# Hybrid decoder layer on one core: later conditioning loads moved and made larger, offsets on the recurrence's products in the planner

## The chip, the cores and the metric

The kernel runs on one core of a Trainium2 chip. The metric is device time in microseconds (us); the profile is one execution, taken by the hardware profiler. TensorE (PE) does the matrix products, VectorE (DVE), ScalarE (ACT) and GpSimd (POOL) the rest, and SyncE (SP) issues nearly all DMAs, one after the other from one queue.

## The reference, cut to what matters

One layer over T = 1024 prompt tokens and 8 sample tokens (1032 columns), D = 1024, float32:

```python
mod = silu(c) @ w_ada + b_ada              # shift1, scale1, gate1, shift2, scale2, gate2
h = rms_norm(x) * (1 + scale1) + shift1
u_glu, qkv_raw, z, b_raw, a_raw, gate_a, gate_b = split(h @ w_in)
# branch A: GLU -> causal depthwise conv (31) -> LayerNorm -> silu -> w_conf_out
# branch B: conv (4) + silu on q, k, v -> gated delta rule, 8 heads of 128 x 128
#           -> rms_norm * silu(z) -> w_gdn_out
merged = sigmoid(gate_a) * y_a + sigmoid(gate_b) * y_b
x = x + gate1 * (merged @ w_o)
h2 = rms_norm(x) * (1 + scale2) + shift2
x = x + gate2 * (relu(h2 @ w_ff1) ** 2 @ w_ff2)
```

The samples have states of their own (the last rows of both convolutions, and one delta matrix for each head), which are read and written back.

## The kernel before, in words

Every large product is done with operands split into a high and a low part (`hi`, `lo`): three products, hi*hi, hi*lo and lo*hi, stand for one. A weight tile comes as 256 KB pieces `raw` (two for an input projection tile); ACT casts each to `whi`, POOL subtracts to get `wlo`. A tile of 128 outputs by 1032 tokens is 72 matmuls of 344 columns (`mm`), in groups of three.

The order of the program is not written by hand. The code records operations (`Op`) with a priority (`plan.prio`, lower goes first), and `Plan.run` plays them through on estimated costs: an engine that is free takes the ready operation of the lowest priority whose tiles fit in their rings. What comes out is a fixed order for each engine, and the chip runs each in that order, with semaphores between engines. If an input is later on the chip than in the plan, the engine stands there, and everything behind it too. `ready` sets when an operation counts as ready (`op.avail`): the end of the latest predecessor and a gap by engine.

Tiles live in rings: `P4`, 34 slots of 4 KB a partition (large tiles), `P2`, 21 slots of 2 KB, and `PS`, the eight PSUM banks. `caps` says how many slots a class may take.

The work in the order of the span:

- Input norm, transposes, and the first part of the conditioning (`ada_first`, 32 loads `wk` of 256 KB), which gives shift1 and scale1. The shifted `h` (`Hh`, `Hl`) is complete at about 57 us.
- The input projection, 56 tiles: for each head k, q and v (`qkv_tile`), the conformer's two (`conformer`), and gates z, gb, ga. Between them the recurrence: 16 units (`unit`: 8 heads, two halves), each one long chain of small products and evictions: transposes (`tT`), `kq`, a triangular inverse in steps (`i16`, `i32`, `j32`, `j64`, `k64`, `k64b`, `k128`; the profile cuts the numbers off, so `i`, `j`, `k`), and four steps of `py`, `pd`, `pw` (each with `po`, the output) that carry the state. PE has dense matmuls of the projection in between, as the plan puts them.
- `ba`, `cum`, `cumT`: decay sums that each unit needs, through DRAM (`scrG`, `Gb`, `glb`).
- `ada_round(1)` and `(2)`: the rest of the conditioning, 64 loads `wk` of 256 KB in the small ring (class `raw`, nine slots, the same as for weights), priority 900. Its result `modT` is first used in the output projection.
- Convolution of 31 taps on DVE (`conf_conv`), the samples' delta step (`pks`, `s0`, `delta_sample`), LayerNorm sums (`pmean`, `pvar`).
- `w_gdn_out` products, `w_conf_out` products, the output projection `w_o` in token quarters (0, 2 and then 1, 3), with `norm2` behind it: `hr` (normed rows), and `parts` of sums and differences (`t1`, `t2`, `bp`) for the feed-forward, which is two products by a seven-product scheme (`ff`), from about 1260 us to the end.

All engine calls go through one line of `Plan.run`, so the profile shows every instruction at one line (469), and one goes by names: out<-in.

Of the kernel before, what the change touches and what calls it, by code (L numbers as in the profile page):

```python
# [10 lines left out]
ALU = mybir.AluOpType  # L11
AX = mybir.AxisListType
# [126 lines left out]


class Op:
    __slots__ = ("alts", "prio", "idx", "tiles", "preds", "succs", "npred", "avail", "start", "eng", "fin", "table", "done", "soft")


ENG = ("PE", "ACT", "DVE", "POOL", "SP")
HOP = 0.4
GAP = {"SP": 0.95, "DVE": 0.127, "POOL": 0.1, "ACT": 0.15}
TABLE = {AF.Exp: "exp", AF.Silu: "silu", AF.Tanh: "", AF.Sqrt: "sqrt"}

# [8 lines left out]
class Plan:  # L158
# [60 lines left out]
    def add(self, alts, reads, writes):  # L219

        op = Op()
        op.alts, op.prio, op.idx, op.done = alts, self.prio, self.n, False
        self.n += 1
        op.preds, op.succs, op.tiles, op.table = set(), [], [], None
        for calls, _ in alts.values():
            for m, a, k in calls:
                if m == "activation":
                    f = a[2] if len(a) > 2 else k.get("func")
                    op.table = TABLE.get(f) or None
        seen = set()  # L230
        for w, refs in ((False, reads), (True, writes)):
            for r in refs:
                for q, box, qw in r.t.acc:
                    if (w or qw) and q is not op and _overlap(box, r.box):
                        op.preds.add(q)
        for w, refs in ((False, reads), (True, writes)):
            for r in refs:
                if w:
                    r.t.acc = [x for x in r.t.acc if not all(c <= a and b <= d for (a, b), (c, d) in zip(x[1], r.box))]
                r.t.acc.append((op, r.box, w))  # L240
                if r.t not in seen:
                    seen.add(r.t)
                    op.tiles.append(r.t)
                    r.t.left += 1
        for t in self.touch:
            if t not in seen:
                seen.add(t)
                op.tiles.append(t)
                t.left += 1
        self.touch = ()  # L250
        op.soft = set(self.after) - op.preds
        op.preds.update(self.after)
        self.after = ()
        self.last = op
        op.preds = [q for q in op.preds]
        self.ops.append(op)
        return op
# [80 lines left out]
    def run(self, name=""):  # L338
# [12 lines left out]
        def ready(op):  # L351
            nonlocal seq
            op.avail = 0.0
            for q in op.preds:
                if q in op.soft:
                    op.avail = max(op.avail, q.start)
                    continue
                same = len(op.alts) == 1 and q.eng in op.alts and q.eng != "SP"
                op.avail = max(op.avail, q.fin + (0.0 if same and q.eng == "PE" else GAP.get(q.eng, HOP)))
            seq += 1  # L360
            heapq.heappush(events, (op.avail, seq, op))
            if len(op.alts) == 1:
                for e in op.alts:
                    soon[e].append(op)
# [11 lines left out]
        while todo:  # L376
# [8 lines left out]
            for e in ENG:  # L385
# [4 lines left out]
                for x in cand[e]:  # L390
# [3 lines left out]
                    k = x.prio  # L394
                    if e == "ACT" and x.table and self.tab and x.table != self.tab:
                        k += self.switch
                    k = (k, x.idx)
# [13 lines left out]
                op = best  # L411
# [46 lines left out]
        for op in sorted(order, key=lambda o: (o.start, o.idx)):  # L458
            for x in op.tiles:
                if x.ap is None:  # L460
                    ring, i = x.slot
# [5 lines left out]
            h = self.hw[op.eng]  # L467
# [13 lines left out]
def hybrid(tc, I, O):  # L481
    nc = tc.nc
    with ExitStack() as ctx:
        ctx.enter_context(tc.manual_schedule())

        def pool(name, space=None, st=ctx, **k):
# [11 lines left out]
            xin=("P4", 16), u=("P4", 8), wk=("P2", 15), h=("P4", 16), w=("P4", 4), wl=("P4", 8), sqa=("P2", 4), rawq=("P4", 2), qkv=("P4", 6),  # L498
            gt=("P4", 3), glu=("P4", 1), av=("P4", 1), avl=("P4", 4), s0=("P4", 3), a=("P4", 8), o=("P4", 16),
            g=("P4", 16), x1=("P4", 8), h2=("P4", 28), hr0=("P4", 6), hr1=("P4", 6), wc=("P4", 7), wd=("P4", 8), wo=("P4", 6), fb=("P4", 18), bp=("P2", 4),  # L500
            acc=("P4", 10), cs=("P4", 2), ff=("PS", 8),
            raw=("P2", 9), Gb=("P2", 2), ktok=("P2", 2), vtok=("P2", 1), att=("P2", 2), Dm=("P2", 1),
            Am=("P2", 1), kqs=("P2", 4), otok=("P2", 2), oT=("P2", 2), tmp=("P2", 12), one=("P2", 19), sq=("P2", 3), lsq=("P2", 4))
        for c, n in dict(jk=2, A32=1, Ad=1, Ao=2, Ac=1, Tc=1, Tb=2, T32=1, Tt=2, Pt=2, Ut=1, R=2, vn=2, Sn=3, st=2, s8=8,
# [123 lines left out]
        def ada_round(r):  # L628
            ps = bank("x", "ada")
            for c in range(4):  # L630
                cols = slice(c * 128, c * 128 + 128)
                for k in range(8):
                    wk = tl("raw", [128, 4, 128], "wk")
                    SP.dma_start(wk, I["w_ada"][4 * r + c, k].rearrange("p (j n) -> p j n", j=4))
                    if k == 0 and c == 0:
                        plan.touch = (ps,)
                    with plan.group("PE"):
                        for j in range(4):
                            TE.matmul(ps[32 * j:32 * j + 32, cols], lhsT=cT[:, k, :], rhs=wk[:, j], start=(k == 0), stop=(k == 7),
                                      tile_position=(0, 32 * j))  # L640
            mo = tl("one", [128, 512], "mo")
            copy(mo, ps)
            ps2 = bank("x", "adaT")
            for c in range(4):
                TE.transpose(ps2[:, c * 128:(c + 1) * 128], mo[:, c * 128:(c + 1) * 128], ident)
            V.tensor_tensor(
                modT[:, 16 * r - 16:16 * r, :].rearrange("p (j c) b -> p j c b", c=4),
                ps2.rearrange("p (c j b) -> p j c b", c=4, j=4)[:, :, :, 0:9],
                bada[:, 16 * r:16 * r + 16].rearrange("p (j c) -> p j c", c=4).unsqueeze(3).to_broadcast([128, 4, 4, 9]),
                ALU.add)  # L650
# [188 lines left out]
        for t in Ub:  # L839
            P.memset(t, 0.0)  # L840

        pk_last = [None]

        def qkv_tile(m, c, i):
            raw = tl("rawq", [128, SL], "rawq")
# [242 lines left out]
            (mm_k if (c, i) == ("ga", 7) else mm)(hi, lo, 8, hx, lambda ns, ps, n: A.activation(gt[:, ns], ps, func, scale=scl))  # L1088
            A.dma_start(spl[c][i], gt)

        plan.prio = 60
        cstT = tl("cs", [128, 4, 8, 30], "cstT")
        plan.after = (ada_op,)
        SP.dma_start(cstT, I["csT"])
        for i in range(4):
            V.tensor_tensor(cstT[:, i], cstT[:, i], cdw[:, 0:30, i].unsqueeze(1).to_broadcast([128, 8, 30]), ALU.mult)
        csS = const([128, 4, 8], "csS")
        V.tensor_reduce(csS, cstT, axis=AX.X, op=ALU.add)
        V.tensor_scalar(cdw, cdw, 0.5, None, op0=ALU.mult)

        av_op = [None]
        conv_after = ()
# [27 lines left out]
            SP.dma_start(aD[i], av)  # L1130
            av_op[0] = plan.last

        plan.prio = 3000
        plan.after = (ada_op,)
        SP.dma_start(O["conf_old"], I["state_conf_conv"][0, :, 1:30, :])
        plan.after = (ada_op,)
        SP.dma_start(O["qkv_old"], I["state_qkv_conv"][0, :, 1:3, :])
        for h in range(H):
            plan.prio = 100 * h + 25
            cur = [qkv_tile(b + h, c, h) for b, c in ((8, "k"), (0, "q"), (16, "v"))]  # L1140
            plan.prio = 100 * h + 20
            for hf in range(2):
                unit(h, hf, cur[1], cur[0], cur[2])
# [164 lines left out]
        plan.prio = 2500  # L1308
        w_g = I["w_gdn_out"]
        for m in range(8):  # L1310
            hi, lo = wload(w_g[m], 8, after=(chain[0],))

            def ev(ns, ps, n):
                sb = tl("tmp", [128, NG], "sb")
# [91 lines left out]
        def norm2(q):  # L1406
# [9 lines left out]
            for i in range(2):  # L1416
# [5 lines left out]
                if q == 3:  # L1422
                    us, ks = r[:, :, e:QW], slice(4 * i, 4 * i + 4)
                    V.tensor_tensor(us, us, s2[:, ks, 1:9], ALU.mult)
                    V.tensor_tensor(us, us, modT[:, 8 + 4 * i:12 + 4 * i, 1:9], ALU.add)
                SP.dma_start(x1D[q][i], x1[q][i])
            sh = [128, 4, QW]
            if q < 2:
                hB[c][1] = parts("h2", hr[0, 0], sh)
# [382 lines left out]
```

## Time and profile before

| | |
|---|---|
| median of 3 runs | 1948.68 us (1948.6 to 1950.59) |
| the profiled execution | 1951.48 us, span 1949.8 us |
| PE, DVE, ACT, POOL busy | 94%, 74%, 44%, 44% |
| DMA | 261.47 MB, mean 134 GB/s |
| granted PE clock, mean | 0.979 |

A wait is read like this: the profile counts an engine as idle before an instruction and names what released it ("2.07 <-DVE xa": idle for 2.07 us until DVE's `xa` was done). A matmul counts as busy longer than the time after which the next one can start, so short waits do not show.

### The profile page before, as it was taken

What the parts mean: (1) busy time and instruction counts of PE and PEld (TensorE: products, weight loads), DVE (VectorE), ACT (ScalarE), POOL (GpSimd) and SP (SyncE); (2) the same over time, 40 slices, a digit from 0 to 9 for tenths busy, and PEclk for the clock granted to TensorE, in tenths of its full rate; (3) what the DMA queues carried; (4) which work ended last, traced back from release to release, by engine and by line L of the source; (5) the groups of instructions that cost most, each with busy time, mean ns of one, the idle gap of its engine ahead of it and who ended that gap; (6) DMA issues with size and microseconds to landing.
All of it is one profiled execution on the core that took longest, in us unless ns stands there. A gap on an engine that the chain in (4) does not pass through costs nothing. (4 is left out here: it accounts for less than half of the span.)

```text
span 1949.8 us, 42076 instructions
## 1 busy us (share of the span) xinstructions
PE 1835.7 (94%) x16205; PEld 1752.1 (90%) x16205; DVE 1439.5 (74%) x3127; ACT 852.6 (44%) x2100; POOL 853.8 (44%) x735
## 2 busy tenths in 40 slices
PE   7899889998999899999999999899999999999995
PEld 4899778988888787999989999889999999999995
DVE  5414457777878998899964485985656677999997
ACT  5323334454545544621142125465555565343334
POOL 3313224354534644363323134422222238888874
PEclk9999899998999999999999999899999999999998
DMA  9441332011111103973254666234544574544432
GB/s 363 118 156 59 103 99 78 30 45 57 41 39 58 67 21 138 339 244 118 107 194 145 187 179 209 98 120 129 163 132 139 161 256 137 177 162 155 131 120 87
DMA packets 164700, 261.47 MB, mean 134 GB/s; under 512 B 27764, under 2 KB 91388, under 8 KB 164484
## 3 DMA queue, kind: packets, MB, share of 16 engines
q1 hardware_dynamic: 158740, 241.91, 38.7%
q10 hardware_dynamic: 5760, 16.88, 2.2%
q8 instruction: 127, 2.08, 0.4%
q14 instruction: 73, 0.60, 0.1%
HBM read 189.76 MB, written 69.64 MB: 133 GB/s over the span
## 5 line engine op out<-in xcount | busy, mean ns | idle before, releaser
L469 PE MATMUL mm<-h_hi,whi 128*128 128x344 f32 x1344 | 462.9, 344 | 4.5 <-ACT whi L469 4.5
L469 PE MATMUL mm<-h_hi,wlo 128*128 128x344 f32 x1344 | 434.7, 323 | 4.6 <-POOL wlo L469 4.4
L469 PE MATMUL mm<-h_lo,whi 128*128 128x344 f32 x1344 | 434.0, 323 | 0.3 <-DVE h_lo L469 0.3
L469 POOL TENSOR_TENSOR wlo<-raw,whi 128x512 fp32r<-128x512 f32 x168 | 248.7, 1495 | 334.7 <-ACT whi L469 242.8
L469 PE MATMUL ff<-fbh,wp 128*128 128x258 f32 x1808 | 331.0, 284 | 3.5 <-DVE accu L469 1.7
L469 PE MATMUL ff<-bp,wp 128*128 128x258 f32 x2688 | 326.7, 284 | 3.9 <-DVE bp L469 1.9
L469 PEld LDWEIGHTS ff<-bp,wp 128*128 128x128 f32 x2688 | 324.9, 190 | 5.4 <-DVE bp L469 2.1
L469 PEld LDWEIGHTS ff<-fbh,wp 128*128 128x128 f32 x1808 | 281.6, 190 | 7.0 <-DVE accu L469 2.8
L469 PEld LDWEIGHTS mm<-h_hi,whi 128*128 128x128 f32 x1344 | 256.5, 191 | 15.5 <-ACT whi L469 5.4
L469 PEld LDWEIGHTS mm<-h_hi,wlo 128*128 128x128 f32 x1344 | 255.9, 190 | 7.7 <-POOL wlo L469 7.6
L469 PE MATMUL ff<-fbl,wp 128*128 128x258 f32 x904 | 256.4, 284 | 2.4 <-DVE fbl L469 2.4
L469 PEld LDWEIGHTS mm<-h_lo,whi 128*128 128x128 f32 x1344 | 257.0, 191 | 0.5 <-DVE h_lo L469 0.5
L469 POOL TENSOR_TENSOR wp<-raw,wp 128x512 fp32r<-128x512 f32 x93 | 141.6, 1528 | 233.7 <-ACT wp L469 227.5
L469 DVE SCALAR_TENSOR_TENSOR av<-gl,vecs,av 128x1024 f32<-128x1024 f32 x120 | 183.4, 1528 | 2.3
L469 PEld LDWEIGHTS ff<-fbl,wp 128*128 128x128 f32 x904 | 171.5, 190 | 2.8 <-DVE fbl L469 2.8
L469 ACT CAST wp<-raw 128x512 fp32r<-128x512 f32 x159 | 95.6, 615 | 134.4 <-PE ff L469 55.2
L469 POOL TENSOR_TENSOR fbl<-fbl,fbh 128x516 fp32r<-128x516 f32 x100 | 149.4, 1528 | 9.8 <-issue 7.7
L469 ACT CAST whi<-raw 128x512 fp32r<-128x512 f32 x168 | 98.9, 619 | 115.0 <-DMA raw<-w_gdn_out 46.8
L469 DVE TENSOR_TENSOR ft<-ff,ft 128x258 f32<-128x258 f32 x160 | 67.4, 422 | 92.2 <-PE ff L469 91.2
L469 ACT ACTIVATE ft<-ft 128x258 f32<-128x258 f32 x224 | 93.4, 419 | 73.4 <-DVE ft L469 69.5
L469 PE MATMUL mm<-g_hi,whi 128*128 128x258 f32 x256 | 75.1, 293 | 6.8 <-ACT whi L469 5.4
L469 POOL TENSOR_TENSOR wp<-s,wp 128x512 fp32r<-128x512 f32 x31 | 51.1, 1650 | 68.1 <-ACT wp L469 68.1
(397 smaller groups left out, 3605.3 us busy)
## 6 DMA issues: line engine op xcount, KB each, us to landing
raw<-w_ff SPq DMA_DIRECT2D x128, 256.0 KB, 4.4
fD<-ft SPq DMA_DIRECT2D x228, 129.0 KB, 3.0
fbl<-fD SPq DMA_DIRECT2D x57, 516.0 KB, 3.6
raw<-w_in SPq DMA_DIRECT2D x112, 256.0 KB, 4.7
wk<-w_ada SPq DMA_DIRECT2D x96, 256.0 KB, 5.1
raw<-w_o SPq DMA_DIRECT2D x32, 256.0 KB, 3.9
sp_z<-gt ACTq DMA_DIRECT2D x8, 516.0 KB, 8.3
zt<-sp_z SPq DMA_DIRECT2D x24, 172.0 KB, 4.0
```

The lines of the kernel that those rows point to most:

```text
L469: getattr(h, m)(*[x.real() if isinstance(x, Ref) else x for x in a], **{q: x.real() if isinstance(x, Ref) else x for q, x in k.items()})
```

## The change

Five edits:

- The planner gives a product's non-PE inputs an offset (`MARGIN`, by the name of the tile written, 0.4 us for dense matmuls and the units' products, 1 to 5 us for others): such a product counts as ready that much later. It holds for PE operations of priority 10 to 2450 and for those of priority -2 and below. The plan puts other work in front; no wait is added on the chip.
- `ada_round` loads 32 pieces of 512 KB (two k blocks each) into two tiles of the large ring (class `ada`), held until the first head's v projection has been issued (`v_op`), with 16 products to a piece. The conformer state `csT` and the two state copies (`conf_old`, `qkv_old`) wait for the same.
- The first `w_gdn_out` tile is loaded at priority 2300 in place of 2500.
- The `parts` of `norm2(0)` and `norm2(2)` get priority 2701 in place of 2690, behind the output projection (2700); those of `norm2(1)` and `norm2(3)` stay at 2691.
- `op.margin` is one more field of `Op`.

```diff
+MARGIN = dict(cum=4.0, cumT=2.0, ada=5.0, adaT=2.0, sn=2.0, pdot=2.0, pks=3.0, pksT=1.0, son=2.0, vrT=2.0, pmean=4.0, pvar=4.0,
+              mm=0.4, **{n: 0.4 for n in ("tT", "kq", "i16", "i32", "j32", "j64", "k64", "k64b", "k128", "pw", "py", "pd", "po")})
...
+        late = "PE" in alts and not -2 < self.prio < 10 and self.prio < 2450
+        op.margin = max([MARGIN.get(r.t.name, 0.0) for r in writes], default=0.0) if late else 0.0
...
-                op.avail = max(op.avail, q.fin + (0.0 if same and q.eng == "PE" else GAP.get(q.eng, HOP)))
+                gap = 0.0 if same and q.eng == "PE" else GAP.get(q.eng, HOP)
+                op.avail = max(op.avail, q.fin + gap + (op.margin if q.eng != "PE" else 0.0))
...
-            acc=("P4", 10), cs=("P4", 2), ff=("PS", 8),
+            acc=("P4", 10), cs=("P4", 2), ff=("PS", 8), ada=("P4", 2),
...
-                for k in range(8):
-                    wk = tl("raw", [128, 4, 128], "wk")
-                    SP.dma_start(wk, I["w_ada"][4 * r + c, k].rearrange("p (j n) -> p j n", j=4))
+                for k2 in range(4):
+                    wk = tl("ada", [128, 2, 4, 128], "wk")
+                    plan.after = (v_op[0],)
+                    SP.dma_start(wk, I["w_ada"][4 * r + c, 2 * k2:2 * k2 + 2].rearrange("k p (j n) -> p k j n", j=4))
...
+        def conf_state():
+            cstT = tl("cs", [128, 4, 8, 30], "cstT")
+            plan.after = (v_op[0],)
+            SP.dma_start(cstT, I["csT"])
...
             cur = [qkv_tile(b + h, c, h) for b, c in ((8, "k"), (0, "q"), (16, "v"))]
+            if h == 0:
+                v_op[0] = pk_last[0]
+                plan.prio = 160
+                conf_state()
+                plan.prio = 3000
+                for o, i in (("conf_old", I["state_conf_conv"][0, :, 1:30, :]), ("qkv_old", I["state_qkv_conv"][0, :, 1:3, :])):
+                    plan.after = (v_op[0],)
+                    SP.dma_start(O[o], i)
...
         for m in range(8):
+            plan.prio = 2300 if m == 0 else 2500
             hi, lo = wload(w_g[m], 8, after=(chain[0],))
+            plan.prio = 2500
...
                 SP.dma_start(x1D[q][i], x1[q][i])
+            plan.prio = 2701 if c == 0 else 2691
             sh = [128, 4, QW]
```

What this does to the orders, at three places. First SP's queue in the opening, from the last loads of `ada_first` (`wk` ahead of and behind `alb`) to the decay sums' copies; `raw` is a piece of a projection weight. Before:

```order
L469 DMA alb<-ab 128x16
L469 DMA wk<-w_ada 128x512 x20
L469 DMA raw<-w_in 128x512 x2
L469 DMA cstT<-csT 128x960
L469 DMA conf_old<-state_conf_conv 8x14848
L469 DMA wk<-w_ada 128x512
L469 DMA qkv_old<-state_qkv_conv 8x6144
L469 DMA raw<-w_in 128x512 x4
L469 DMA wk<-w_ada 128x512 x6
L469 DMA scrS<-sab 8x16
```

Now, at the same place:

```order
L475 DMA alb<-ab 128x16
L475 DMA wk<-w_ada 128x512 x3
L475 DMA raw<-w_in 128x512 x2
L475 DMA wk<-w_ada 128x512 x6
L475 DMA raw<-w_in 128x512 x8
L475 DMA scrS<-sab 8x16
```

Nine of the `wk` belong to `ada_first` in both; the other eighteen, `csT` and both state copies have left this place, and four more weight pieces stand in it.

Second PE in a unit, the step from `py` to `pd` (DVE's `vn` lies between them) at the start of the fourth head's recurrence. Before:

```order
L469 MATMUL py<-vtok,U_78 128x128
L469 MATMUL mm<-h_hi_694,whi 128x344
L469 MATMUL mm<-h_lo_709,whi 128x344
L469 MATMUL mm<-h_hi_694,wlo 128x344
L469 MATMUL mm<-h_hi_780,whi 128x344
L469 MATMUL mm<-h_lo_800,whi 128x344
L469 MATMUL mm<-h_hi_780,wlo 128x344
L469 MATMUL pd<-vn,ktok 128x128
```

Now:

```order
L475 MATMUL py<-vtok,U_78 128x128
L475 MATMUL mm<-h_hi_709,whi 128x344
L475 MATMUL mm<-h_lo_724,whi 128x344
L475 MATMUL mm<-h_hi_709,wlo 128x344
L475 MATMUL mm<-h_hi_768,whi 128x344
L475 MATMUL mm<-h_lo_784,whi 128x344
L475 MATMUL mm<-h_hi_768,wlo 128x344
L475 MATMUL mm<-h_hi_779,whi 128x344
L475 MATMUL mm<-h_lo_792,whi 128x344
L475 MATMUL mm<-h_hi_779,wlo 128x344
L475 MATMUL pd<-vn,ktok 128x128
```

Three groups of dense matmuls lie between the two where there were two. Over all units the median is 6 matmuls before and 9 now, for py to pd, pd to pw and pw to py alike. Before, 864 dense matmuls come ahead of the first `kq` and 2790 ahead of the last `po`; now 357 and 2736. The 32 larger `wk` come late: four ahead of the first head's `delta_prompt` store, 28 behind the fourth head's, the last two behind the samples' `scrV`.

Third DVE in the output projection: `hr`, `t1`, `t2` and `bp` are parts of `norm2(2)`, `x1` and `gs` are evictions of w_o's products. Before:

```order
L469 TENSOR_TENSOR t2_14932<-hr_14799,t1_14877 128x1032
L469 TENSOR_TENSOR hr_14756<-hr_14799,hr_14756 128x1032
L469 TENSOR_TENSOR bp_14917<-t1_14877,bp_14916 128x1032
L469 TENSOR_TENSOR bp_14952<-t2_14932,bp_14951 128x1032
L469 TENSOR_TENSOR bp_14972<-hr_14756,bp_14971 128x1032
L469 TENSOR_TENSOR hr_14833<-hr_14833,t2_14932 128x1032
L469 TENSOR_TENSOR bp_14938<-hr_14799,bp_14937 128x1032
L469 TENSOR_TENSOR x1_30_14847<-gs_14853,xr_14740 128x8
L469 SCALAR_TENSOR_TENSOR x1_30_14847<-mm_14823,modT_2206,xr_14827 128x250
```

Now:

```order
L475 TENSOR_TENSOR t2_14910<-hr_14735,t1_14862 128x1032
L475 TENSOR_TENSOR sqa_14700<-sqa_14700,sq_14905 128x258
L475 SCALAR_TENSOR_TENSOR x1_30_14783<-mm_14854,modT_8861,xr_14858 128x250
L475 TENSOR_TENSOR gs_14940<-mm_14854,modT_8861 128x8
L475 TENSOR_TENSOR hr_14692<-hr_14735,hr_14692 128x1032
L475 TENSOR_TENSOR x1_30_14783<-gs_14940,xr_14858 128x8
L475 SCALAR_TENSOR_TENSOR x1_10_14687<-mm_14898,modT_8861,xr_14902 128x258
L475 TENSOR_TENSOR bp_14934<-t2_14910,bp_14933 128x1032
```

Evictions and parts take turns, where eleven parts in a row stood ahead of the next eviction.

More of the change, by code (lines that the diff above doesn't have):

```diff
@@ L141 @@
 class Op:
-    __slots__ = ("alts", "prio", "idx", "tiles", "preds", "succs", "npred", "avail", "start", "eng", "fin", "table", "done", "soft")
+    __slots__ = ("alts", "prio", "idx", "tiles", "preds", "succs", "npred", "avail", "start", "eng", "fin", "table", "done", "soft", "margin")
 ENG = ("PE", "ACT", "DVE", "POOL", "SP")
 HOP = 0.4
+MARGIN = dict(cum=4.0, cumT=2.0, ada=5.0, adaT=2.0, sn=2.0, pdot=2.0, pks=3.0, pksT=1.0, son=2.0, vrT=2.0, pmean=4.0, pvar=4.0,
+              mm=0.4, **{n: 0.4 for n in ("tT", "kq", "i16", "i32", "j32", "j64", "k64", "k64b", "k128", "pw", "py", "pd", "po")})
 GAP = {"SP": 0.95, "DVE": 0.127, "POOL": 0.1, "ACT": 0.15}
@@ L631, in ada_round @@
                 cols = slice(c * 128, c * 128 + 128)
-                for k in range(8):
-                    wk = tl("raw", [128, 4, 128], "wk")
-                    SP.dma_start(wk, I["w_ada"][4 * r + c, k].rearrange("p (j n) -> p j n", j=4))
-                    if k == 0 and c == 0:
+                for k2 in range(4):
+                    wk = tl("ada", [128, 2, 4, 128], "wk")
+                    plan.after = (v_op[0],)
+                    SP.dma_start(wk, I["w_ada"][4 * r + c, 2 * k2:2 * k2 + 2].rearrange("k p (j n) -> p k j n", j=4))
+                    if k2 == 0 and c == 0:
                         plan.touch = (ps,)
                     with plan.group("PE"):
-                        for j in range(4):
-                            TE.matmul(ps[32 * j:32 * j + 32, cols], lhsT=cT[:, k, :], rhs=wk[:, j], start=(k == 0), stop=(k == 7),
-                                      tile_position=(0, 32 * j))
+                        for k in (2 * k2, 2 * k2 + 1):
+                            for j in range(4):
+                                TE.matmul(ps[32 * j:32 * j + 32, cols], lhsT=cT[:, k, :], rhs=wk[:, k % 2, j], start=(k == 0),
+                                          stop=(k == 7), tile_position=(0, 32 * j))
             mo = tl("one", [128, 512], "mo")
@@ L840, in hybrid @@
             P.memset(t, 0.0)
-        pk_last = [None]
+        pk_last, v_op = [None], [None]
         def qkv_tile(m, c, i):
@@ L1089, in gate @@
             A.dma_start(spl[c][i], gt)
[L1091 to L1096, printed above, removed]
-        csS = const([128, 4, 8], "csS")
-        V.tensor_reduce(csS, cstT, axis=AX.X, op=ALU.add)
-        V.tensor_scalar(cdw, cdw, 0.5, None, op0=ALU.mult)
+        csS = const([128, 4, 8], "csS")
+        def conf_state():
+            cstT = tl("cs", [128, 4, 8, 30], "cstT")
+            plan.after = (v_op[0],)
+            SP.dma_start(cstT, I["csT"])
+            for i in range(4):
+                V.tensor_tensor(cstT[:, i], cstT[:, i], cdw[:, 0:30, i].unsqueeze(1).to_broadcast([128, 8, 30]), ALU.mult)
+            V.tensor_reduce(csS, cstT, axis=AX.X, op=ALU.add)
+            V.tensor_scalar(cdw, cdw, 0.5, None, op0=ALU.mult)
         av_op = [None]
@@ L1131, in conf_conv @@
             av_op[0] = plan.last
[L1133 to L1137, printed above, removed]
         for h in range(H):
```

## The prediction

> **What bounds the kernel now.** I read the page first, then the stretches of the span, then TensorE's waits stretch by stretch, and last the timeline around the longest waits.
>
> ```profile
> span 1949.8 us, 42076 instructions
> PE 1835.7 (94%) x16205; PEld 1752.1 (90%) x16205; DVE 1439.5 (74%) x3127; ACT 852.6 (44%) x2100; POOL 853.8 (44%) x735
> ```
>
> TensorE (PE) is busy 94% of the span, every other engine 74% or less. The change removes no product, so it can only win where PE waits or runs at a lowered clock. The stretches say where that is; the columns are stretch, length, busy time of each engine, granted PE clock, DMA share and GB/s.
>
> ```profile
> 57.20:300.00 242.80, 221.83 (x1949) 209.53 (x1946) 103.43 (x230) 75.26 (x191) 67.83 (x81) 0.96 0.32 97
> 300.00:800.00 500.00, 465.65 (x5291) 422.47 (x5290) 408.17 (x1234) 254.63 (x781) 235.81 (x259) 0.97 0.20 67
> 1200.00:1250.00 50.00, 43.00 (x325) 41.82 (x324) 46.88 (x60) 31.73 (x59) 27.73 (x18) 0.90 0.49 160
> ```
>
> PE idles 242.80 - 221.83 = 21.0 us in the opening of the projections, 34.4 us while the recurrence's units run (300 to 800 us), and 7.0 us in the 50 us around the switch to the second half of the output projection. So about 62 us of idle time lie where the change acts; the feed-forward from 1260 us on it leaves alone. There is a second cost in the same places, the granted clock:
>
> ```profile
> 668.70 0.44 PE L469 MATMUL j<-Tt,Am 32*32 32x32 f32 x16 [2.04 <-DVE Tt L469]
> 669.80:673.20 3.40, 3.40 (x27) 2.96 (x26) 2.76 (x8) 3.32 (x8) 3.15 (x2) 0.50 0.03 5
> 671.65 0.49 PE L469 MATMUL mm<-h_lo,whi 128*128 128x344 f32 x1
> 671.94 0.49 PE L469 MATMUL mm<-h_hi,wlo 128*128 128x344 f32 x1
> ...
> 69.44 0.32 PE L469 MATMUL mm<-h_hi,whi 128*128 128x344 f32 x1
> 69.60 0.32 PE L469 MATMUL mm<-h_lo,whi 128*128 128x344 f32 x1
> ```
>
> After a wait of 2.04 us the clock was 0.50 for 3.4 us, and dense matmuls started 0.29 us apart where at full clock it is 0.16 (0.158 over long runs). So half of the busy time in such a stretch is lost. These stretches, grouped (opening; units, first and last of six; output projection), are
>
> ```profile
> sum 20.40, PE 12.34 PEld 11.40 DVE 10.71 ACT 7.66 POOL 15.13; mean PE 4.11 PEld 3.80 DVE 3.57 ACT 2.55 POOL 5.04
> ...
> 328.50:331.90 3.40, 3.40 (x43) 2.96 (x42) 3.05 (x9) 2.04 (x2) 3.23 (x3) 0.50 0.02 5
> 680.00:683.40 3.40, 3.40 (x17) 3.28 (x17) 2.53 (x9) 0.59 (x2) 0.91 (x2) 0.50 0.40 153
> sum 27.20, PE 26.21 PEld 23.09 DVE 21.98 ACT 15.17 POOL 20.91; mean PE 4.37 PEld 3.85 DVE 3.66 ACT 2.53 POOL 3.48
> 1233.00:1243.20 10.20, 6.15 (x27) 5.86 (x28) 10.20 (x21) 5.08 (x11) 4.68 (x4) 0.50 0.73 230
> ```
>
> which is 12.34 / 2 = 6.2 us, 26.21 / 2 = 13.1 us and 6.15 / 2 = 3.1 us lost. The Trainium skill (TensorE: Matmul & The Clock Gate, Part 1) says that the gate closes after at least one idle window of about 3.4 us. By that page only waits of 3.4 us and more would cost clock, the clock terms below would be some 6 us in place of 17, and the sum would give 1905 us. The row above, half clock right behind 2.04 us, decides here, and the sum goes by the rows.
>
> **The change part by part.**
>
> *The opening (57 to 300 us).* Its waits:
>
> ```profile
> PE i L469 <- DVE Tt L469: 11.2, 2, 6.8
> PE mm L469 <- ACT whi L469: 3.7, 2, 3.1
> PE cum L469 <- DVE xa L469: 2.1, 1, 2.1
> PE ada L469 <- DMA wk<-w_ada: 2.0, 1, 2.0
> PE mm L469 <- POOL wlo L469: 1.9, 3, 0.8
> ...
> 202.65 1.69 PE L469 MATMUL kq<-kqs 128*128 128x256 f32 x12
> ...
> 215.59 0.65 PE L469 MATMUL i<-Tt,Ao 32*32 32x32 f32 x32 [6.78 <-DVE Tt L469]
> ...
> GB/s 363 118 156 59 103 99 78 30 45 57 41 39 58 67 21 138 339 244 118 107 194 145 187 179 209 98 120 129 163 132 139 161 256 137 177 162 155 131 120 87
> ```
>
> SP's rows now have ten weight pieces between alb and the small scrS to Gb copies, where six stood, and no second-part conditioning load among them; before, 18 of those stood there (4.7 MB at the first slice's 363 GB/s, 13 us of the queue). I let the whi and wlo waits at 84 to 86 us (3.1 + 0.8) go. `cum` has 75 matmuls between baT and itself, where 48 stood: 27 x 0.158 = 4.3 us more cover against a wait of 2.1, so it goes. The `ada` wait goes, since its product is moved far behind. The first unit's `i` wait (6.8) stands in a place where only `ada` products were left to run; the order now has 90 dense matmuls (14.2 us) there against a chain of 215.6 - 202.7 = 12.9 us, so it goes. The second unit's (11.2 - 6.8 = 4.4) and the waits for weights around 270 us shrink; I take half, 3.1. Sum 3.9 + 2.1 + 2.0 + 6.8 + 3.1 = 17.9 us, and of the clock's 6.2 us I take 4.8 (all but half of the last stretch). **-22.7 us**; bounds 8 (only cum, weights and ada) and 27.
>
> *The units (300 to 800 us).* Waits of PE there, the first seven of 18 rows (38 waits, 33.7 us in all):
>
> ```profile
> PE i L469 <- DVE Tt L469: 5.5, 5, 1.9
> PE pd L469 <- DVE vn L469: 4.6, 5, 2.9
> PE pw L469 <- DVE Sn L469: 3.9, 4, 1.5
> PE j L469 <- DVE Tt L469: 3.8, 4, 2.0
> PE i L469 <- ACT jk L469: 3.2, 1, 3.2
> PE k L469 <- DVE U L469: 2.8, 3, 1.4
> PE k L469 <- ACT Ut L469: 2.1, 2, 1.9
> ```
>
> They are hops of one chain (product, eviction on DVE or ACT, next product), and PE fills each with dense matmuls. The order's medians rise from 6 to 9 matmuls for py to pd, pd to pw and pw to py alike, 3 x 0.158 = 0.474 us more cover for each hop. A wait shown is also short by some 0.16 us, since a matmul counts as busy for 0.32 but the next may start after 0.16. Cutting each of the 38 by up to 0.474 gives 17 us. Of the clock's 13.1 us I take 9: four of the six stretches follow waits of about 2 us or less, which fall under the 2.04 of the row above, and two (3.2 and 2.9 us) stay. **-26 us**; bounds 0 (each wait comes back whole) and 53 (all 33.7, the hidden 6 and 13.1 go). The dense matmuls needed for this are there: in the order 2379 stand between the first unit's kq and the last unit's po, where 1926 did, and the units start after 357 of them instead of 864.
>
> *The output projection (1200 to 1250 us).* PE's long wait there and what holds it:
>
> ```profile
> 1236.44 0.58 PE L469 MATMUL mm<-g_hi,whi 128*128 128x258 f32 x1 [5.00 <-ACT whi L469]
> SPq L469 <- DVE sqa L469: 18.1, 1, 18.1
> L469 DVE TENSOR_TENSOR bp<-t,bp 128x1032 fp32r<-128x1032 f32 x2 | 4.6, 2325 | 0.0
> L469 DVE SCALAR_TENSOR_TENSOR x<-mm,modT,xr 128x250 f32<-128x250 f32 x1 | 0.5, 464 | 0.0
> ```
>
> SP stood 18.1 us behind DVE, with the next w_o pieces queued behind it; DVE was in a run of 128x1032 parts of up to 2.3 us each, ahead of the evictions. The new priority (2701 for the first half's parts, behind the 2700 of the evictions) puts an eviction after every two or three parts. The parts are due later only by the evictions' 0.46 us each; if they came too late, the first products of the feed-forward would wait for them, which is the upper bound of this term. I take 8 of 7.0 + 3.1; bounds +5 (the 5.0 us come back at the feed-forward) and -10. **-8 us.**
>
> *The layer norm's sums.* 4 us offsets on pmean and pvar, with 51 dense matmuls between them instead of 21:
>
> ```profile
> PE pmean L469 <- DVE sm L469: 1.0, 1, 1.0
> PE pvar L469 <- DVE sm L469: 0.5, 1, 0.5
> ```
>
> **-1 us**, of bounds 0 and 1.5.
>
> *Conditioning loads late.* 64 pieces of 256 KB become 32 of 512 KB in two tiles of the large ring; 28 of them are issued behind the fourth head's last unit. They hold SP's queue when a tile is not free, and the weights queue behind them. The busiest slice behind that place:
>
> ```profile
> raw<-w_in SPq DMA_DIRECT2D x8, 256.0 KB, 10.8
> 750.00:800.00 50.00, 48.84 (x584) 42.98 (x585) 41.83 (x132) 23.11 (x67) 9.57 (x10) 1.00 0.49 168
> 800.00:850.00 50.00, 50.00 (x321) 49.98 (x320) 49.79 (x79) 27.53 (x79) 24.99 (x15) 1.00 0.93 340
> ```
>
> At a DMA share of 0.93 weight pieces took 10.8 us to land and PE still did not wait. The 20 pieces nearest to it (10.5 MB, 31 us at 340 GB/s) mostly fall in front of that slice, where the share is 0.49 and less. Bounds 0 and 31 (all of it exposed); I take a little, **+3 us**, since the products have a 5 us offset as well. The conformer state, and the two state copies, move with them at no cost: the DMA share of 0.20 over 300 to 800 us hides them; without that cover their 1.2 MB (by their shapes) are 3 us at 363 GB/s.
>
> *W_gdn_out's first piece ahead* (priority 2300): PE shows no wait for it before, so 0; the `of` and `zt` loads behind it come 0.5 MB, 1.5 us, later, which the gates' dense products hide; if not, it is 1.5 us. The first 57 us: the dense run starts after 78 matmuls instead of 60 (-2.8 us), but the last first-part load stands behind 0.5 MB more (+1.4); I take 0.
>
> Sum: -22.7 - 26 - 8 - 1 + 3 = -55 us. The profiled execution took 1951.48 us for a span of 1949.8, and the median of the runs is 1948.68, so the execution lies 0.14% above it; the sum taken off the median gives **1894 us**.
>
> **The rivals.**
>
> *DVE is the real bound of the units.* In 300 to 800 us it is busy 408 of 500; if it runs behind its order by as much as PE is given, each wait returns and only the opening, the sums and the output projection pay: 1949 - 22.7 - 8 - 1 + 3 = 1920 us. Against it: with 453 more dense matmuls in the stage (72 us) DVE's share falls to about 408 / 572 = 71%.
>
> *Everything goes.* 27 + 53 + 10 + 1.5 = 91.5: 1857 us. Waits of 3 us, longer than the new cover, speak against it.
>
> *The offsets shift the waits and cover none, the first unit's included.* Then cum, the weights, half of the output projection: 1949 - 2.1 - 3.9 - 5 = 1938 us. If these do not come either, no change is measured (within 0.2%, 3.9 us, about what a measurement of this kernel can tell).
>
> *Slower: late loads in lockstep.* Two tiles let only two pieces fly; SP waits for PE's product to free one, and weights queue behind. If each piece cost what the wait for wk at 208 us did (2.0, and 1.7 of clock), 32 x 3.7 = 118 us, and the time is 1949 - 55 + 118 = 2012. It decides from 15 pieces on (55 / 3.7); with 20 it is 1968 us. The low DMA share ahead of 800 us speaks against it.
>
> **How the numbers follow.** Near the sum, 1872 to 1912: 0.65. DVE the bound (1912 to 1930): 0.13. Everything goes (under 1872): 0.09. Shift only (1930 to 1944): 0.05. No change: 0.03. Slower: 0.05. Faster is 0.65 + 0.13 + 0.09 + 0.05 = 0.92. The range 1864 to 1928 leaves out the ends of the first, the last and the shift-only case, and somewhat under 0.2.
>
> **What would show it.** In the profile after: PE idle in the unit stage near 17 us in place of 34, with fewer stretches at 0.50; no wait of `i` over 3 us in the first unit; `cum` without a wait; no 18 us hold of SP near 1220 us and no 5 us wait of whi; wk landing by 850 us without a PE wait for `ada`. I am wrong if PE's waits in the units keep their sum (DVE), or if waits for whi, wlo or wk grow after 650 us.

## The result and the profile after

The changed kernel takes 1897.04 us (median of 4 runs, 1895.96 to 1897.81) against 1949.63 us for the kernel before on the same chip: a ratio of 0.9728, with an interval from 0.9712 to 0.9744. The forecast was 1894. The profiled execution took 1896.7 us for a span of 1895.0.

The head of its page:

```profile
span 1895.0 us, 41996 instructions
PE 1819.3 (96%) x16205; PEld 1742.7 (92%) x16205; DVE 1436.5 (76%) x3137; ACT 847.1 (45%) x2089; POOL 856.7 (45%) x734
```

The products are the same 16205. PE's busy time fell by 16.4 us all the same, mostly because it ran at half clock (granted clock 0.50) less often: by the records of the granted clock it was busy for 54.3 us in such stretches before and for 29.2 now, and half of the difference is 12.5 us. The rest of the 54.8 us is idle time. The stretches show where; columns are as before (stretch, length, busy time of PE, PEld, DVE, ACT and POOL, granted PE clock, DMA share, GB/s). Of the kernel before, from 57 us to the end of the last unit:

```profile
57.20:801.60 744.40, 689.08 (x7250) 633.60 (x7246) 513.20 (x1466) 330.56 (x972) 303.64 (x340) 0.97 0.24 77
```

Of the kernel after, nearly the same piece of work (7264 matmuls and 7250), and then the three stretches that the prediction read, the last at its new place:

```profile
57.20:750.50 693.30, 669.69 (x7264) 615.21 (x7262) 535.71 (x1492) 328.80 (x972) 301.63 (x337) 0.99 0.28 90
57.20:300.00 242.80, 231.59 (x2269) 217.29 (x2267) 162.34 (x465) 113.86 (x329) 106.57 (x123) 0.97 0.21 62
300.00:800.00 500.00, 487.60 (x5313) 447.41 (x5313) 422.31 (x1105) 238.29 (x709) 223.59 (x229) 0.99 0.38 130
1150.00:1200.00 50.00, 42.91 (x328) 41.82 (x326) 48.68 (x59) 28.10 (x56) 33.95 (x21) 0.93 0.44 150
```

Up to the last unit PE idled 744.40 - 689.08 = 55.3 us before and 693.30 - 669.69 = 23.6 us now. The clock rose from 0.97 to 0.99. The stretch around the switch in the output projection is no better: 7.1 us idle of 50, where it was 7.0.

PE's waits in the kernel after, first from 57.2 to 300 us (four of five rows), then from 300 to 800 us (the first four of nine rows; all nine are 12.0 us, where it was 33.7):

```profile
PE j L475 <- DVE Tt L475: 5.2, 1, 5.2
PE mm L475 <- POOL rawq L475: 3.4, 1, 3.4
PE py L475 <- DVE R L475: 1.1, 1, 1.1
PE tT L475 <- ACT qkvq L475: 0.9, 1, 0.9
...
PE pw L475 <- DVE Sn L475: 2.7, 3, 1.2
PE i L475 <- DVE Tt L475: 2.2, 1, 2.2
PE pd L475 <- DVE vn L475: 2.0, 4, 0.7
PE j L475 <- DVE Tt L475: 1.8, 1, 1.8
```

The group of `kq`, the first product of each unit (shortest, median and longest in ns, then the first and the last start), shows that the units begin at 103.9 us, where it was 202.65:

```profile
L475 PE MATMUL kq<-kqs x192: 274/281/388, 103.9 to 690.0; 128*128 128x256 f32 x192
```

And the output projection: PE's long waits at the switch, and SP's waits from 1160 to 1210 us:

```profile
1182.69 0.38 PE L475 MATMUL mm<-g_hi,whi 128*128 128x258 f32 x1 [1.51 <-ACT whi L475]
1185.76 0.58 PE L475 MATMUL mm<-g_hi,wlo 128*128 128x258 f32 x1 [2.56 <-POOL wlo L475]
1200.50 0.70 PE L475 MATMUL ss<-sqa,ones 128*128 128x258 f32 x2 [3.01 <-DVE sqa L475]
...
SPq L475 <- DVE x L475: 31.4, 3, 15.4
```

The 5.0 us wait for `whi`, and 2.0 us for `wlo` beside it, became three waits that add up to 7.1 us, and SP is still held behind DVE, now behind the evictions `x`.

### The profile page after: what moved, and what is told of

Its sections match the earlier page's. It is cut to its first block, busy times and chain, and to the rows that moved or that the text cites. A ratio compares the mean times of both kernels' runs of the same rounds, so it can differ in the third digit from the quotient of the medians.

```text
span 1895.0 us, 41996 instructions
## 1 busy us (share of the span) xinstructions
PE 1819.3 (96%) x16205; PEld 1742.7 (92%) x16205; DVE 1436.5 (76%) x3137; ACT 847.1 (45%) x2089; POOL 856.7 (45%) x734
## 5 line engine op out<-in xcount | busy, mean ns | idle before, releaser
L475 DVE SCALAR_TENSOR_TENSOR av<-gl,vecs,av 128x1024 f32<-128x1024 f32 x120 | 181.7, 1514 | 1.9
L475 ACT ACTIVATE gt<-mm 128x344 f32<-128x344 f32 x72 | 32.1, 457 | 112.9 <-PE mm L475 88.1
```

The source lines that it names most:

```text
L475: getattr(h, m)(*[x.real() if isinstance(x, Ref) else x for x in a], **{q: x.real() if isinstance(x, Ref) else x for q, x in k.items()})
```

## The experiments

All times are medians. Ratios are to the kernel before in the same session; it stood at 1946.7 to 1949.6 us.

**The parts alone.** First the planner's offsets by themselves, on the kernel before:

```diff
+MARGIN = dict(cum=4.0, ..., mm=0.4, **{n: 0.4 for n in (...)})
+                op.avail = max(op.avail, q.fin + gap + (op.margin if q.eng != "PE" else 0.0))
```

> The kernel before with the products' offsets alone; the conditioning loads, the state copies, the first w_gdn_out tile and the parts stand as before. Theory (offsets and loads pay apart, each where the prediction put it): the units' waits shrink by the added cover and the clock's part with them, cum loses its wait, and the waits for weights near 84 us and for wk stay: 1949 - 26 - 2 - 1 = 1920 us. Rival 1 (the offsets pay only because the held loads let the units start early and spread DVE's work): 1940 us or more. Rival 2 (the offsets are the whole gain): 1900 us or less.

Measured: 1971.91 us, ratio 1.0111 (1.009 to 1.0132). It is slower by some 22 us. The theory and the second rival miss; the first rival's range (1940 us or more) holds it, but none of the three forecast a loss. The waits from 1004 to 1062 us show where much of it lies: PE stands there for DVE's `o_lo`, an input of the w_gdn_out products, above all:

```profile
PE mm L474 <- DVE o_lo L474: 7.6, 5, 4.6
```

From 1004.8 to 1063.0 us PE idles 11.9 us, at a mean clock of 0.85.

Then the loads alone: the changed kernel without offsets, and with the old priorities of the first w_gdn_out tile and of the parts.

```diff
-                op.avail = max(op.avail, q.fin + gap + (op.margin if q.eng != "PE" else 0.0))
+                op.avail = max(op.avail, q.fin + gap)
-            plan.prio = 2300 if m == 0 else 2500
-            plan.prio = 2701 if c == 0 else 2691
```

> The changed kernel with offsets of zero, and the w_gdn_out tile and the parts at their old priorities: the moved and larger conditioning loads alone. Theory: the opening's term alone, less a little for late loads: 1949 - 21 + 3 = 1931 us, with PE's waits in the units as in the kernel before (6 dense matmuls to a hop). Rival 1 (an early start of the units spreads DVE's work, and the waits go without offsets): 1910 us or less. Rival 2 (the loads are worth nothing by themselves): 1945 us or more.

Measured: 1932.42 us, 0.9913 (0.9898 to 0.9928), the time that the theory had (1931). So the parts give +22 and -17 us, and together, with the two priorities, -53: they are not a sum. This run also has a wait that the change as a whole has not (PE's row, then the stretch around it):

```profile
788.64 0.66 PE L475 MATMUL mm<-h_hi,whi 128*128 128x344 f32 x1 [8.34 <-ACT whi L475]
...
765.00:800.00 35.00, 24.66 (x140) 23.65 (x139) 34.84 (x52) 13.05 (x36) 16.29 (x11) 0.85 0.97 344
```

This is not the mechanism that the prediction's slower case named: the last `wk` of this kernel is issued at 719.1 us and the last `ada` product starts at 730.3. The transfers of the stretch are weights, the samples' states, and rows of z and o. The weight pieces issued from 768.5 to 778.9 us landed some 5 to 6 us later, but ACT's next cast of one started only at 784.8, by the profile behind DVE's convolution (`av`), while DVE is busy for 34.84 of the 35 us:

```profile
784.78 0.62 ACT L475 CAST whi<-raw 128x512 fp32r<-128x512 f32 x1 [5.57 <-DVE av L475]
```

In the change the DMA is as full (0.98 from 750 to 800 us) and PE has no wait, so a full DMA alone does not make one.

Two small edits taken out one at a time, the parts' priority (back to 2690):

> The changed kernel with the parts of norm2 at their old priorities (2690 and 2691). Theory from the two traces (the stage from the first g_hi product to the first feed-forward product took 110.3 us before and 111.4 after, the next 42 us of the feed-forward lost 2.2 us less): the edit is worth 2 to 4 us, so 1900 us. The prediction's term: 8 us, so 1905. Rival (it only moves waits): 1897 us, the same.

and the first w_gdn_out tile's (back to 2500):

> The changed kernel with the first w_gdn_out tile at its old priority 2500. Theory: PE shows no wait at the first o_hi product in either trace, so 1897 us, the same within 1 us. Rival (the tile ahead is what keeps PE busy at the turn from the gates): 1899 us or more, with a wait for whi at the first o_hi product.

Measured: 1899.96 us (0.9745, 0.973 to 0.9759) and 1898.87 us (0.974, 0.9724 to 0.9756). Neither is told apart from the change's 0.9728. Without the tile's early load PE waits at the first products of the stage, as the rival said, and in the change it does not:

```profile
956.22 0.43 PE L475 MATMUL mm<-o_hi,whi 128*128 128x344 f32 x1 [1.56 <-ACT whi L475]
957.62 0.42 PE L475 MATMUL mm<-o_hi,wlo 128*128 128x344 f32 x1 [0.82 <-POOL wlo L475]
```

Without the parts' priority the output projection is 2.0 us shorter (109.4 against 111.4 from the first product of g to the first of the feed-forward) and the first half of the feed-forward 4.5 us longer (330.6 against 326.1).

**Which offsets.** On the changed kernel, the 0.4 us offsets at zero:

```diff
-              mm=0.4, **{n: 0.4 for n in (...)})
+              mm=0.0, **{n: 0.0 for n in (...)})
```

> The changed kernel with the 0.4 us offsets of the dense matmuls and of the units' products at zero; the larger ones (1 to 5 us: ada, cum, pmean and so on) stay. PE then has again a median of 6 dense matmuls between a unit's products. Theory, small and large offsets both pay, each in its own place: without the small ones the units and the opening lose about 16 us more (the held loads alone left 125.3 + 30.8 us lost there, against 110.2 + 29.7 for the change), while the weight wait of 8.3 us and the slow clock around 780 us, which the held loads alone had, stay away: about 1913 us. Rival A, the large offsets alone mend the held loads (all of the 35 us between 1932 and 1897): about 1899 us. Rival B, the small ones alone do: about 1930 us, with the whi wait near 788 us back.

Measured: 1915.13 us, 0.9839 (0.9823 to 0.9855). The theory had about 1913. The small offsets are worth 18 us here by the medians and 22 by the ratios, and the other 17 or 14 us to the loads alone are of the larger ones and the two priorities. The long wait near 788 us is away, though from 772 to 803 us two waits for `whi` and two for `wlo` stay, of 2.7 us each pair.

On the kernel before, the larger offsets alone and the small ones alone:

> The kernel before with the larger offsets only (1 to 5 us: cum, ada, pmean and so on). 792 dense matmuls ahead of the first kq, 3063 ahead of the last po (2790 before), a median of 6 between a unit's products. Theory, the loss of the offsets alone (22 us) comes from dense matmuls used up before the recurrence ends; with 3063 some are left, so the w_gdn_out stage loses little and the units wait as before: about 1952 us, from 1945 to 1960. Rival, the offset on ada is what does harm (its products move behind the first units and stand in their way): 1965 us or more.

> The kernel before with the 0.4 us offsets of the dense matmuls and the units' products only. 864 dense matmuls ahead of the first kq, 3162 ahead of the last po, a median of 9 between a unit's products. Theory, the cover of the units returns some 15 us, and the end of the recurrence, which comes at a later dense matmul, gives about as much back in the w_gdn_out stage (waits for o_lo and o_hi): 1945 us, from 1935 to 1958. Rival, the small offsets are the harmful ones: 1965 us or more, with 15 us or more lost in the w_gdn_out stage.

Measured: 1972.44 us, 1.0128 (1.0109 to 1.0146), and 1950.42 us, 1.0016 (1.0005 to 1.0028). So in the kernel before the larger offsets do all the harm, and the small ones, worth some 20 us in the change, are worth nothing there (0.16% slower). The second run is the key to the case. PE's wait before the layer norm's sums, in the kernel before and with the small offsets:

```profile
1003.90 2.00 PE L469 MATMUL pmean<-sm,ones 128*128 128x344 f32 x6 [0.99 <-DVE sm L469]
```

```profile
1003.23 3.81 PE L473 MATMUL pmean<-sm,ones 128*128 128x344 f32 x6 [20.96 <-DVE sm L473]
```

With the small offsets PE had done all products of the input projection 20.7 us sooner (981.9 in place of 1002.6) and then stood 21 us for `sm`, which DVE finished at the same time as ever.

Could PE have done w_gdn_out's products in that time, had the plan put them ahead of `pmean`? No: DVE finishes their input `o_lo` at 999.3 us, and their first weight is cast from 999.2 on.

```profile
998.81 0.52 DVE L473 TENSOR_TENSOR o_lo<-of,o_hi 128x344 fp32r<-128x344 f32 x1
```

The kernel with all offsets alone has that order, and there PE stands for `o_lo` instead, as shown above. The stretch from the last `po` to the wait for `sm`, before, with the small offsets, with the larger ones, and after (here to the end of `sm`):

```profile
801.50:1003.90 202.40, 198.01 (x1249) 195.97 (x1248) 182.64 (x196) 62.46 (x156) 81.53 (x47) 1.00 0.57 202
```

```profile
842.90:1003.20 160.30, 137.88 (x877) 137.32 (x875) 152.17 (x141) 36.87 (x82) 61.51 (x35) 0.94 0.48 170
```

```profile
850.50:1030.30 179.80, 161.93 (x991) 159.35 (x990) 171.57 (x213) 59.24 (x152) 67.06 (x39) 0.95 0.61 218
```

```profile
750.40:961.60 211.20, 211.20 (x1346) 211.18 (x1346) 162.25 (x182) 61.95 (x150) 87.11 (x50) 1.00 0.54 192
```

DVE (the third busy time) is busy for 90, 95 and 95% of it, and 77% in the change. What it does there is above all the convolution (DVE's largest group in three of these stretches: before, with the small offsets, after):

```profile
L469 DVE SCALAR_TENSOR_TENSOR av<-gl,vecs,av 128x1024 f32<-128x1024 f32 x89 | 140.9, 1584 | 2.2
```

```profile
L473 DVE SCALAR_TENSOR_TENSOR av<-gl,vecs,av 128x1024 f32<-128x1024 f32 x77 | 116.4, 1512 | 1.9
```

```profile
L475 DVE SCALAR_TENSOR_TENSOR av<-gl,vecs,av 128x1024 f32<-128x1024 f32 x71 | 113.6, 1600 | 1.7
```

Of its 120 operations 89 stood behind the last unit before, and PE had just enough gate products to cover them: 1.0 us of wait. DVE's busy time from the start to the end of `sm` is 723 to 737 us in all fourteen kernels (729.3 up to 1003.9 us before, 733.4 after), so that end moves only if DVE gets its work sooner or idles less. In the change the recurrence begins 99 us sooner, DVE has 70.7 us of work from 104 to 203 us in place of 31.6, and 68.3 us from 203 to 300 in place of 53.0, and `sm` is ready at 961.6. PE has used up the products of the input projection at 955.1, but `o_lo` is ready too, w_gdn_out's products stand ahead of `pmean`, and PE does not wait:

```profile
964.38 1.90 PE L475 MATMUL pmean<-sm,ones 128*128 128x344 f32 x6
```

With the larger offsets DVE stands still early (two of its waits from 200 to 400 us, larger offsets, then before):

```profile
DVE glu L474 <- PE mm L474: 26.8, 3, 14.6
DVE qkvk L474 <- ACT rawq L474: 21.7, 1, 21.7
```

```profile
DVE qkvk L469 <- ACT rawq L469: 6.7, 1, 6.7
DVE glu L469 <- PE mm L469: 5.3, 2, 3.3
```

That is 36.5 us more, and DVE is busy for 96.8 of these 200 us, where it was 130.3; `sm` comes at 1030 us, 26 us later, and the whole is 25.6 us longer. The rival had the size; that `ada`'s offset does it was not tried by itself. The small offsets' time lies in the range of its theory (1935 to 1958 us), by another wait than it named. My theory of both expectations, that dense matmuls are used up, named only the cover and not the engine that was behind.

**Hold or ring.** The loads held as in the change, but as 64 pieces of 256 KB in the ring of the small tiles (the size of the pieces changes with the ring, and the two were not tried apart):

```diff
-                    wk = tl("ada", [128, 2, 4, 128], "wk")
+                    wk = tl("raw", [128, 4, 128], "wk")
```

> The changed kernel with the later conditioning loads held back as in the change, but as 64 pieces of 256 KB in the small ring that the weights use too. Theory, holding them back is what opens the front (units start about 100 us sooner), and ring and size matter little: 1897 us, up to 1903, first kq near 104 us. Rival, the ring matters: late pieces take slots of the weights' ring, the weights come late behind the last head's units, and PE waits for whi or wlo between 700 and 960 us: 1910 us or more.

And in the large ring, but not held (the conformer state and the state copies still are):

```diff
-                    plan.after = (v_op[0],)
```

> The changed kernel with the later conditioning loads in 512 KB pieces in the large ring as in the change, but not held: they may go as soon as a tile is free. 792 dense matmuls stand ahead of the first kq (357 in the change, 864 before). Theory, both halves are needed (hold alone opened the front but its 64 pieces came in one block and gave 1939 us; ring alone spreads the pieces but does not open the front): first kq near 195 us, last po past 820 us, and as with the offsets alone the w_gdn_out stage then waits for its inputs: 1950 to 1975 us. Rival A, the ring alone does it all: within 8 us of the change, 1889 to 1905 us. Rival B, the ring does half (no waits for weights in the units, but a late start): about 1925 us.

Measured: 1939.16 us, 0.9963 (0.9948 to 0.9977), and 1927.28 us, 0.9895 (0.9878 to 0.9911). I had expected the hold to be nearly all of it, and then the ring without it to be worth nothing; both were wrong, and the second time rival B was right (about 1925 us, half). With the offsets in all four, the ratio is 1.0111 with neither (that kernel has the two old priorities too), 0.9963 with the hold alone, 0.9895 with the ring alone and 0.9728 with both: each gives 1.5 to 2.4%, with or without the other.

What the small ring costs is not what the rival said (weights late behind the last units) but this:

```profile
160.00:220.00 60.00, 50.68 (x600) 32.28 (x598) 4.86 (x17) 6.91 (x27) 3.06 (x3) 0.80 0.70 245
```

With nine slots the pieces go in one block once the hold ends (nine issues up to 154 us, the other 55 from 175 to 218). For 60 us SP's queue brings them and little else, 460 of PE's 600 matmuls are `ada` products, at a mean clock of 0.80, and DVE is busy for 4.9 us: the recurrence, begun at 103.4 us, nearly stands still. The last `po` comes 50 us later than in the change (800.5). Two tiles of the large ring put 4 pieces in that place and 28 behind the fourth head's units, a few products at a time.

What the missing hold costs: first `kq` at 182.5 us, last `po` at 838.9, and before one of the last units

```profile
794.00 0.65 PE L475 MATMUL i<-Tt,Ao 32*32 32x32 f32 x32 [12.54 <-DVE Tt L475]
...
780.00:795.00 15.00, 1.65 (x37) 1.39 (x38) 14.71 (x50) 5.49 (x15) 6.70 (x7) 0.55 0.60 226
```

where DVE, busy for 14.71 of 15 us, holds up PE: late again.

How much of its work DVE gets early goes with the end of `sm`. From 104 to 300 us (DVE is the third busy time), before, with the hold alone, with the ring alone, and in the change:

```profile
104.00:300.00 196.00, 181.02 (x1646) 170.23 (x1645) 84.62 (x186) 62.70 (x164) 56.12 (x68) 0.96 0.31 100
```

```profile
104.00:300.00 196.00, 178.22 (x1876) 150.14 (x1875) 93.34 (x263) 61.25 (x168) 56.53 (x69) 0.90 0.36 122
```

```profile
104.00:300.00 196.00, 181.65 (x1704) 170.64 (x1702) 116.04 (x275) 74.67 (x209) 78.28 (x87) 0.94 0.24 79
```

```profile
104.00:300.00 196.00, 185.68 (x1973) 171.78 (x1971) 138.93 (x413) 91.91 (x269) 87.65 (x104) 0.97 0.15 49
```

Their `sm` ends at 1004.7, 1004.0, 995.1 and 961.6 us. So the early first `kq` of the hold alone (103.4 us) does not bring that end forward by itself. These are four kernels in one order, and no run moved DVE's work by itself.

**More of it.** 0.8 us in place of both 0.4, then for the units' products only, then 0.6 for those and none for the dense matmuls:

> The changed kernel with 0.8 in place of 0.4 us for the dense matmuls and the units' products. Median of 12 dense matmuls between two products of a unit (9 in the change), and 3162 dense matmuls ahead of the last po (2736). Theory, the offsets win only as long as dense matmuls are left for the gates and the w_gdn_out products behind the recurrence: the units' idle time falls from 22.7 to some 12 us, but the last po comes some 65 us later, and the end of the recurrence then holds up w_gdn_out's inputs as it did with the offsets alone (19.8 us lost in that stage at 3300 matmuls): 1897 - 11 - 3 (clock) + 12 = about 1895 us, between 1885 and 1910, with waits for o_hi or o_lo in the w_gdn_out stage. Rival A, more cover is simply better: 1897 - 11 - 3 = 1883 us, and no wait in the w_gdn_out stage. Rival B, the waits are not shortened by more cover, since DVE and ACT fall behind by as much: 1897 us with 22 us idle in the units and the same last po within 10 us.

> The changed kernel with 0.8 us for the units' products only (tT, kq, i, j, k, pw, py, pd, po); the dense matmuls keep 0.4. 3105 dense matmuls ahead of the last po. Theory: as with 0.8 for both, since the units' products set the spacing: within 5 us of that kernel. Rival A: the dense matmuls' own offset is what matters (a weight's half that comes late), then this one stays at 1897 us while the other moves.

> The changed kernel with 0.6 us for the units' products and none for the dense matmuls (0.4 and 0.4 in the change). 3171 dense matmuls ahead of the last po. Theory: 0.8 for both gave 1902, 0.8 for the units with 0.4 for the dense ones 1893; the dense matmuls' own offset puts one group behind another for a weight's half that comes late, and costs more than it covers; without it the time falls again, to about 1888 us. Rival: between the two values of the units' offset nothing changes and the dense matmuls need their own 0.4 against waits for whi and wlo: 1897 to 1905 us, with more of those waits than the 0.8 and 0.4 kernel had.

Measured: 1902.01 us (0.9768, 0.9754 to 0.9783), 1892.65 us (0.9724, 0.9709 to 0.9738) and 1907.58 us (0.9799, 0.9783 to 0.9814). The first falls into its range but for another reason: the w_gdn_out stage has no wait, and PE's idle time from 104 us to the end of the units is 28.3 us in place of 22.7. The second misses its theory (within 5 us of the first; it is 9 us less). It is the lowest median of all, though its ratio is not told apart from the change's. The third misses too: its theory is wrong, and its largest waits are for DVE's `Tt` (10.3 us, the longest 3.9) and not for weights, so its rival's reason is not shown either. Why the dense matmuls want about 0.4 stays open; each value gives another order of the whole projection.

## Why the prediction was right, and where it was not

- **Opening and units (-22.7 and -26).** Forecast were 17.9 + 17 = 34.9 us of waits and 4.8 + 9 = 13.8 us of clock. Found: 55.3 - 23.6 = 31.7 us of idle time, and the records of the granted clock show 47.8 us of half clock before and 20.5 after from 57.2 us to the last unit (another 3.4 us, at 23.7 us, lie ahead of it). One of the stretches after stands under the clock below; the others are

```profile
119.30:126.10 6.80, 5.85 (x21) 5.79 (x22) 6.42 (x26) 1.29 (x2) 1.14 (x3) 0.50 0.00 0
177.30:184.10 6.80, 4.34 (x43) 3.84 (x44) 4.97 (x8) 4.72 (x9) 5.43 (x5) 0.50 0.22 51
604.00:607.40 3.40, 3.40 (x14) 3.03 (x15) 2.56 (x4) 2.88 (x10) 1.87 (x2) 0.50 0.00 0
```

  In these stretches PE was busy 12.34 + 26.21 = 38.6 us before and 17.0 after, so by the prediction's own measure, half of it, the lost work fell by 10.8 us. The two together come to 42.5 of 48.7 us; the split does not hold. From 57 to 300 us, where the units now run with waits of their own, PE's idle time fell by 9.8 where 17.9 was forecast, and from 300 to 800 us by 22 where it was 17. That these differences make up for each other in part is luck. `cum` and `ada` wait no more, as forecast. The first `i` wait of 6.8 us is gone, but 5.2 us for `j` and 3.4 us for `wlo` came in the first units (the row names POOL's `rawq`, a small operation that follows `wlo` on POOL and ends with the wait).
- **The clock.** Half clock still follows short waits:

```profile
402.20 0.45 PE L475 MATMUL i<-Tt,Ao 32*32 32x32 f32 x32 [2.15 <-DVE Tt L475]
...
402.60:406.00 3.40, 3.40 (x48) 3.01 (x41) 2.37 (x6) 0.45 (x1) 3.04 (x4) 0.50 0.00 0
```

  By the rule of the Trainium skill (TensorE: Matmul & The Clock Gate, Part 1) that a whole idle window of about 3.4 us must pass, waits of this length would have cost no clock and their going would have gained none. The row is against it; the length of the slow stretch, 3.40 us, agrees with the page's window.
- **Layer norm's sums (-1).** Both waits went, 1.5 us. But from the last unit to w_gdn_out PE idled 4.4 us before and 0 now: 3.3 us of that were waits for `wlo` and `whi`, for which the prediction had no term. As the small offsets showed, the 1.0 us for `sm` was the visible end of DVE's queue.
- **Late loads (+3).** 0 us in the change: PE has no wait from 750 to 955 us, and the last `ada` product is at 745.4. So none of its bound of 31 us was met. The 8.3 us wait of the loads alone is no sign of this term: it ends 58 us behind the last `ada` product.
- **w_gdn_out's tile (0).** Without the edit 2.4 us of waits for the tile's weights appear at the stage's first products, which the kernel before did not have; why they come late there is not shown. In the whole it is not told apart from nothing.
- **Output projection (-8).** The step that failed. The projection is 1.1 us longer, the first half of the feed-forward 4.4 us shorter: -3.3, and taken out by itself the edit is not told apart from nothing. Of the signs forecast for it, the 5.0 us wait for `whi` is 1.5, but SP's hold did not go: over the whole projection SP stands behind DVE for 31.4 us, and before it was 18.1 behind `sqa` and 13.3 behind `x`, as much. Putting evictions between the parts shortened the wait for `whi`, and waits for `wlo` (2.6 us) and for DVE's `sqa` (3.0) came at the same switch. DVE is busy for 48.7 of 50 us there, so it has no time to give, and I read this as the order on it only choosing who waits.
- **The sum.** 31.7 + 10.8 + 4.4 + 3.3 = 50 of the span's 54.8 us; the rest I cannot place. It came right partly by luck, with a flaw in the reasoning: I added the cover of the offsets as though PE's waits were all there was. The rival "DVE is the bound" I held to be unlikely by DVE's mean share, 71% by my estimate (79% in fact, 513.29 of 650.5 us from 100 to 750.5). With the small offsets alone that rival was true, not inside the units where I had put it but behind them. What made the offsets pay, as I read the runs, was that DVE's chain got its work sooner, and for the whole of it both the hold and the ring were needed; my terms counted for it only PE's waits in the opening. That the earlier DVE is the reason rests on the traces; a run that makes DVE's work shorter and changes nothing else is missing.

## What to carry to other kernels

Before adding up an engine's waits as a gain, look at the stretch just ahead of the next point where all engines meet: if a second engine is busy for nearly all of it, as DVE was from the last unit to `sm` (90 to 95%), waits that are taken away can come back in one piece at that point, until the second engine gets its work sooner. Test the parts of a change apart and together, since here +22 and -17 made -53. And where loads are held back, the ring that they go to is their schedule: here two slots of 512 KB spread them, and nine of 256 KB let them go in one block that held up everything behind them in the queue.

## What was not expected of the hardware

The convolution's operation of one shape (128x1024, `av<-gl,vecs,av`) took between 1.24 and 2.38 us in the change, and 1.60 us in the mean behind the last unit:

```profile
L475 DVE SCALAR_TENSOR_TENSOR av<-gl,vecs,av x120: 1241/1285/2383, 546.0 to 894.6; 128x1024 f32<-128x1024 f32 x120
```

The trace says more. Of the 120 operations, 61 have no POOL instruction running beside them, and each of these took 1.24 to 1.29 us; the 59 that overlap one took 1.24 to 2.38 us, with a median of 1.83. All fourteen kernels show the same: none of these operations took over 1.29 us without POOL beside it. Two places in the change, first two operations with POOL idle (2.59 us together), then one beside POOL's `wlo` and `of` (to 808.70 and from 808.67 us):

```profile
800.11 2.59 DVE L475 SCALAR_TENSOR_TENSOR av<-gl,vecs,av 128x1024 f32<-128x1024 f32 x2
807.48 2.31 DVE L475 SCALAR_TENSOR_TENSOR av<-gl,vecs,av 128x1024 f32<-128x1024 f32 x1
```

If POOL is the reason, which no run tried, it costs DVE some 28 us by an estimate from these numbers (181.7 us for the 120, less 120 of 1.28 us). Since DVE's chain bounds the kernel with the small offsets alone, it would be worth trying to keep POOL's work out of the convolution.
